# The norm's weights on ScalarE's queue, and ten warming products placed six and four

## The chip, the cores and the metric

The kernel runs on one core of a Trainium2 chip. The core has TensorE (PE in the profile; PEld is its weight load), VectorE (DVE), ScalarE (ACT), GpSimd (POOL) and SyncE (SP). SyncE only issues transfers here; ScalarE and GpSimd can issue transfers of their own besides computing. The metric is device microseconds for one execution. Three timed runs of the kernel before took 772.16, 772.48 and 773.34 us; the median is 772.48 us.

## The reference

One hybrid decoder layer on x of 256 tokens by 2048 channels, in float32. x is normed, projected by one wide matrix into two token mixers (a gated DeltaNet and an attention, eight heads of 128 each), their outputs are gated, projected, merged, projected again, normed and added to x:

```python
def rms_norm(x, w):
    y = xf * lax.rsqrt(jnp.mean(xf * xf, axis=-1, keepdims=True) + NORM_EPS)
    return (y * w.astype(jnp.float32)).astype(x.dtype)
...
    proj = h @ w_in
    gdn_qkv, gdn_z, gdn_b, gdn_a, moba_qkv, moba_z, gate_a, gate_b = jnp.split(proj, offsets, axis=-1)
...
    h = rms_norm(x, pre_norm_w[l])
    y = hybrid_mixer(h, w_in[l], conv_w[l], a_log[l], dt_bias[l], gdn_norm_w[l],
                     w_branch_a[l], w_branch_b[l], w_out[l])
    x = x + rms_norm(y, post_norm_w[l])
```

Only the first line of the layer matters for the change: `h = rms_norm(x, pre_norm_w)`, and the first columns of `h @ w_in`.

## The kernel before, in words

Every large product splits its float32 operands into a rounded part (`hi`) and the rest (`lo`), and adds three products: hi by hi, hi by lo, lo by hi. ScalarE makes `hi` with a copy, VectorE makes `lo` with a subtraction. `hT` holds the transposed and weighted x, hi in columns 0 to 255 and lo in columns 256 to 511 of each of 16 blocks of 128 channels. The factor 1/rms is applied later, to the products.

The first phase computes the first four heads' keys (`pfirst`, tiles `a_k`) straight from arriving data. Nothing has been loaded when it begins, so it runs as a pipeline over eight chunks of 256 channels (two blocks):

- SyncE's queue issues, in the order of the text: `nrow` (L162: the norm's weights, 16 rows of 128), and then for each chunk two pieces of x (L171, 128 tokens by 256 channels) and two pieces of `w_in` (L173, tile `rawf_k`, 128 channels by 512 columns). The small tables `prow` and `adrow` (L185 to L189) and the later weights (L352 on) come behind these.
- TensorE multiplies a matrix of ones with itself WARM times (L231, tile `warm`; no result is used), transposes `nrow` (L288, tile `pnc`), from which VectorE copies `ncol`, the weights as a column (L289), transposes the four x blocks of chunk 0 (L290, `turn(0)`, tile `hTp`), and multiplies the ones again WARM2 times (L291). A float32 product of 128 columns is two MATMUL rows of the trace; a transpose is one.
- `turned(c)` (L247) makes ScalarE write the hi half of a block of `hT`, scaled by `ncol` (L254), and the hi of the weights (L255), and VectorE the lo half of `hT` (L257) and the lo of the weights (L261), block by block.
- `first_products(k, part)` (L279) is four products with hi of the weights (512 columns, since hT's hi and lo lie side by side) or four with lo (256 columns). For the first two chunks, the next chunk's `turn` and `turned` stand between the first block's hi and lo products, later ahead of both (L295 to L301). `stats` sums the squares of x beside it.

`pin` (L145) keeps pinned instructions of an engine in the order of the text; every TensorE instruction is pinned, and so are the copies and subtractions of `turned` and the copy at L183, which stands at the head of ScalarE's own work. Other instructions may be placed elsewhere on their engine when the program is built. From the second phase on, `proj_t` and `proj_n` stream weights of up to 1 MB through three buffers (`wraw`), in an order written out by hand (`ORDER`), and queues of generators (`tick`) put the small work of the two mixers between the products.

```python
    for i in range(WARM):
        mm(warm[:, :P], ones, ones, start=True, stop=True)
...
    tr(pnc[:, :KT], nrow, ident[:KT, :KT])
    pin(nc.vector.tensor_copy(ncol, pnc[:, :KT]))
    pt = turn(0)
    for i in range(WARM2):
        mm(warm[:, :P], ones, ones, start=True, stop=True)
    turned(0, pt)
```

Of the kernel before, what the change touches and what calls it, by code (L numbers as in the profile page):

```python
# [15 lines left out]
P = 128  # L16
EPS = 1e-6
NEG = -1e30

WARM = 4  # L20
WARM2 = 7
STATS = 1, 2, 4, 5

PG_WAIT = 3.5
# [51 lines left out]
def hybrid_layer(  # L76
# [15 lines left out]
    nc = tc.nc  # L92
# [35 lines left out]
    def aux_tile(name):  # L128
        return aux.tile([P, 512], F32, tag="aux", name=name)
# [17 lines left out]
    def mm(*args, **kwargs):  # L147
        return pin(nc.tensor.matmul(*args, **kwargs))  # L148
# [10 lines left out]
    ZW, ZBA = ZG[3] - ZG[2], GW - ZG[2]  # L159

    nrow = cst.tile([KT, P], F32, name="nrow")
    nc.sync.dma_start(nrow, pre_norm_w.rearrange("o (k p) -> (o k) p", p=P))  # L162
    prow = big.tile([P, P], F32, tag="ga", name="prow")
    xall = big.tile([P, NT, D], F32, tag="u1", name="x")
    xs = [xall[:, t, :] for t in range(NT)]
# [64 lines left out]
    warm = aux_tile("warm")  # L230
    for i in range(WARM):  # L231
        mm(warm[:, :P], ones, ones, start=True, stop=True)
# [5 lines left out]
    def turn(c):  # L238

        pt = aux_tile(f"hTp_{c}")  # L240
        for k in range(2):
            for t in range(NT):
                f = (2 * c + k) * P
                tr(pt[:, k * S + t * P : k * S + (t + 1) * P], xs[t][:, f : f + P], ident)
        return pt
# [44 lines left out]
# [3 lines that stand above are left out]
# [1006 lines left out]
```

## Time and profile before

| what | value |
|---|---|
| median of 3 runs | 772.48 us (772.16 to 773.34) |
| the profiled execution, its own time | 773.75 us |
| its span, first to last instruction | 772.0 us |
| granted TensorE clock over the span | 0.997 |
| TensorE busy (matmuls) | 762.1 us, 99% of the span |
| VectorE, ScalarE, GpSimd busy | 565.5, 435.5, 34.9 us |
| moved by DMA | 151.87 MB, mean 197 GB/s |

The profiled execution took 773.75 us, of which 1.7 us lie outside the span; it is 1.27 us above the median of the timed runs. Times in the views count from the span's start. In a timeline row the first number is the start, the second the stretch that the merged instructions cover, both in us; "x8" is their count; the bracket gives the engine's idle time ahead and what ended it. A row "SPq" is a transfer's issue on SyncE, not the transfer. The clock column tells only what the profile records of the clock's throttle; the durations of equal instructions tell the rate that TensorE ran at.

### The profile page before, as it was taken

The numbers are of one execution on the slowest core, as the hardware profiler recorded it, in microseconds if no ns is written. First come the engines' busy times: TensorE is split into PE (matmuls) and PEld (weight loads), VectorE is DVE, ScalarE is ACT, GpSimd is POOL, SyncE is SP. The second block draws the span as 40 slices with busy tenths as digits, with TensorE's granted clock in tenths as the row PEclk, the third lists the DMA queues.
The fourth block names the chain that finished last, engine by engine and source line by source line (L and its number), as shares of the span: only waits on it lengthen the run. The fifth ranks groups of instructions, "written<-read, shape, count | busy, mean of one in ns | idle before, by whom it ended". The sixth has DMA issues, their size and how long they took to land.

```text
span 772.0 us, 10411 instructions
## 1 busy us (share of the span) xinstructions
PE 762.1 (99%) x3943; PEld 650.8 (84%) x3943; DVE 565.5 (73%) x918; ACT 435.5 (56%) x660; POOL 34.9 (5%) x63
## 2 busy tenths in 40 slices
PE   9999999999999999999999999999999999999995
PEld 8898988899888888888898888788888888888884
DVE  5887769885977898775457876686648676888843
ACT  5777666657655654554456474654455544555731
POOL 4000001112000000003001000000000000000000
PEclk9999999999999999999999999999999999999998
DMA  8576676458565557668437356667545955375912
GB/s 289 181 234 219 182 218 183 137 149 231 184 206 174 190 184 215 172 194 203 135 109 273 126 200 217 229 212 245 197 163 172 372 180 202 112 296 190 339 45 110
DMA packets 94808, 151.87 MB, mean 197 GB/s; under 512 B 3365, under 2 KB 49062, under 8 KB 94246
## 3 DMA queue, kind: packets, MB, share of 16 engines
q1 hardware_dynamic: 90054, 134.42, 53.8%
q0 software_dynamic: 4128, 15.74, 6.1%
q10 hardware_dynamic: 576, 1.05, 0.4%
q8 instruction: 31, 0.51, 0.3%
q14 instruction: 19, 0.16, 0.1%
HBM read 148.04 MB, written 3.15 MB: 196 GB/s over the span
## 4 chain that ended last, share of the span: by engine, by line
PE 96%; ACT 2%; DVE 1%; DMA 0%; issue 0%; DVEq 0%; SPq 0%
PE a_gb L148 11%; PE a_ga L148 11%; PE a_y L148 11%; PE a_zg L148 6%; PE a_k L148 6%; PE a_mq L148 6%; PE a_v L148 6%; PE a_mk L148 6%; PE a_ub L148 6%; PE a_zm L148 6%; PE a_mv L148 5%; PE a_ua L148 5%; PE a_q L148 4%; PE s L148 1%; PE ms L148 1%; PE po L148 1%
## 5 line engine op out<-in xcount | busy, mean ns | idle before, releaser
L148 PE MATMUL a_ga<-hi_ga,hT 128*128 128x512 f32 x256 | 82.1, 394 | 0.0
L148 PE MATMUL a_gb<-hi_gb,hT 128*128 128x512 f32 x256 | 80.2, 390 | 0.0
L227 DVE TENSOR_TENSOR lo_gb<-raw_gb,hi_gb 128x1024 fp32r<-128x1024 f32 x32 | 38.9, 1224 | 25.0 <-ACT hi_gb L226 24.9
L148 PEld LDWEIGHTS a_gb<-hi_gb,hT 128*128 128x128 f32 x256 | 48.0, 188 | 10.5
L148 PEld LDWEIGHTS a_ga<-hi_ga,hT 128*128 128x128 f32 x256 | 48.1, 188 | 10.1
L226 ACT CAST hi_gb<-raw_gb 128x1024 fp32r<-128x1024 f32 x32 | 33.3, 1051 | 35.6 <-PE a_gb L148 26.5
L226 ACT CAST hi_ga<-raw_ga 128x1024 fp32r<-128x1024 f32 x32 | 33.6, 1054 | 32.1 <-PE a_ga L148 13.7
L227 DVE TENSOR_TENSOR lo_ga<-raw_ga,hi_ga 128x1024 fp32r<-128x1024 f32 x32 | 38.9, 1222 | 17.4 <-ACT hi_ga L226 17.2
L148 PE MATMUL a_ga<-lo_ga,hT 128*128 128x512 f32 x128 | 50.1, 392 | 0.1
L148 PE MATMUL a_gb<-lo_gb,hT 128*128 128x512 f32 x128 | 50.1, 391 | 0.0
L148 PE MATMUL a_zg<-hi_zg,hT 128*128 128x348 f32 (+1 forms) x192 | 47.1, 322 | 0.0
L148 PE MATMUL a_mq<-hT,hi_mq 128*128 128x512 f32 x128 | 47.0, 408 | 0.0
L148 PE MATMUL a_mk<-hT,hi_mk 128*128 128x512 f32 x128 | 46.2, 402 | 0.0
L148 PE MATMUL a_y<-hi_y,mT 128*128 128x512 f32 x144 | 46.1, 392 | 0.0
L148 PE MATMUL a_q<-hT,hi_q 128*128 128x512 f32 x128 | 45.9, 398 | 0.0
L148 PE MATMUL a_v<-hT,hi_v 128*128 128x512 f32 x128 | 45.3, 399 | 0.0
L148 PE MATMUL a_k<-hT,hi_k 128*128 128x512 f32 x128 | 41.4, 407 | 0.0
L148 PE MATMUL a_ub<-hi_ub,obT 128*128 128x512 f32 x128 | 41.3, 395 | 0.0
L148 PE MATMUL a_zm<-hi_zm,hT 128*128 128x512 f32 x128 | 40.5, 392 | 0.0
L148 PE MATMUL a_mv<-hi_mv,hT 128*128 128x512 f32 x128 | 40.1, 391 | 0.0
L148 PE MATMUL a_v<-hT,lo_v 128*128 128x256 f32 x128 | 36.0, 281 | 0.0
L148 PE MATMUL a_q<-hT,lo_q 128*128 128x256 f32 x128 | 35.9, 280 | 0.0
(384 smaller groups left out, 1976.6 us busy)
## 6 DMA issues: line engine op xcount, KB each, us to landing
raw_ga<-in_w_in_dram SPq DMA_DIRECT2D x16, 1024.0 KB, 5.1
raw_gb<-in_w_in_dram SPq DMA_DIRECT2D x16, 1024.0 KB, 6.0
raw_y<-in_w_out_dram SPq DMA_DIRECT2D x15, 1024.0 KB, 5.3
raw_q<-in_w_in_dram SPq DMA_DIRECT2D x8, 1024.0 KB, 5.6
raw_mv<-in_w_in_dram SPq DMA_DIRECT2D x8, 1024.0 KB, 5.1
raw_v<-in_w_in_dram SPq DMA_DIRECT2D x8, 1024.0 KB, 5.6
raw_zm<-in_w_in_dram SPq DMA_DIRECT2D x8, 1024.0 KB, 5.0
raw_mq<-in_w_in_dram SPq DMA_DIRECT2D x8, 1024.0 KB, 5.7
```

The source lines that it names most:

```text
L148: return pin(nc.tensor.matmul(*args, **kwargs))
L226: nc.scalar.copy(hi, raw)
L227: nc.vector.tensor_tensor(lo, raw, hi.bitcast(F32), op=ALU.subtract)
```

## The change

The transfer of `nrow` is issued by ScalarE instead of SyncE, so that x's first piece is the first transfer on SyncE's queue. WARM goes from 4 to 6 and WARM2 from 7 to 4: six warming products ahead of the transposes and four behind them, ten in all instead of eleven. Nothing else is edited.

```diff
-WARM = 4
-WARM2 = 7
+WARM = 6
+WARM2 = 4
...
     nrow = cst.tile([KT, P], F32, name="nrow")
-    nc.sync.dma_start(nrow, pre_norm_w.rearrange("o (k p) -> (o k) p", p=P))
+    nc.scalar.dma_start(nrow, pre_norm_w.rearrange("o (k p) -> (o k) p", p=P))
```

## The prediction

> **What bounds the kernel now.** I read the page first (shares, chain), then TensorE's waits, the chain over the first 40 us, and last the first 14 us engine by engine.
>
> ```profile
> span 772.0 us, 10411 instructions
> PE 762.1 (99%) x3943; PEld 650.8 (84%) x3943; DVE 565.5 (73%) x918; ACT 435.5 (56%) x660; POOL 34.9 (5%) x63
> PE 96%; ACT 2%; DVE 1%; DMA 0%; issue 0%; DVEq 0%; SPq 0%
> ```
>
> TensorE is busy 99% of the span and carries 96% of the chain. Its waits over the whole run, and the head of the chain:
>
> ```profile
> PE warm L148 <- DVE epst L182: 1.1, 1, 1.1
> PE hTp L151 <- DMA x<-in_x_dram: 0.7, 1, 0.7
> ...
> 1.27 2.81 DMA x<-in_x_dram
> 4.13 1.27 PE hTp L151 x4
> 5.40 2.99 PE warm L148 x14
> 8.39 1.71 PE a_k L148 x4
> ```
>
> Only two waits stand in the list, both before 4.13 us. So what TensorE does before its first real product (`a_k`, 8.04 us below) lies on the path, and later work follows TensorE. The one stretch later on in which the chain leaves it for long runs from 50.9 to 63.9 us over ScalarE and VectorE; it begins where TensorE's products release it (chain: `a_zg` ends, `hi_q` starts) and moves along with them. Nothing behind 35 us is edited. I therefore forecast the shift of the first phase and carry it to the end undiminished.
>
> TensorE's rows of that phase, weight loads left out but for one:
>
> ```profile
> 1.14 2.08 PE L148 MATMUL warm<-ones 128*128 128x128 f32 x8 [1.14 <-DVE epst L182]
> 3.15 0.28 PE L151 MATMUL pnc<-ident,nrow 16*128 16x16 f32 x1
> 4.13 1.27 PE L151 MATMUL hTp<-ident,x 128*128 128x128 f32 x4 [0.70 <-DMA x<-in_x_dram]
> 4.50 0.50 PEld L151 LDWEIGHTS hTp<-ident,x 128*128 128x128 f32 x3 [0.19 <-DMA x<-in_x_dram]
> 5.20 3.19 PE L148 MATMUL warm<-ones 128*128 128x128 f32 x14
> 8.04 2.05 PE L148 MATMUL a_k<-hT,hi_k 128*128 128x512 f32 x4
> 9.89 0.68 PE L151 MATMUL hTp<-ident,x 128*128 128x128 f32 x4
> 10.33 0.72 PE L148 MATMUL a_k<-hT,lo_k 128*128 128x256 f32 x4
> 10.88 1.08 PE L148 MATMUL a_k<-hT,hi_k 128*128 128x512 f32 x4
> 11.80 0.64 PE L148 MATMUL a_k<-hT,lo_k 128*128 128x256 f32 x4
> 12.27 1.09 PE L148 MATMUL a_k<-hT,hi_k 128*128 128x512 f32 x4
> ...
> L148 PE MATMUL warm<-ones x22: 421/421/580, 1.1 to 8.0; 128*128 128x128 f32 x22
> ```
>
> Four hi products take 2.05 us at 8.04 and 1.08 at 10.88: TensorE runs at half rate until about 10.0 us and at full rate from there. The third hi group, at 12.27, is my marker; what it gains, the run gains. The work from the first product to the marker, at full rate, is two hi groups of 0.92 (10.88 to 11.80), two lo groups of 0.47 (11.80 to 12.27) and four transposes of 0.44 (9.89 to 10.33): 3.22 us. Check: 1.96 us at half rate do 0.98 of it, and 12.27 minus 10.0 is 2.27, together 3.25.
>
> **The change part by part.** *Warming products.* Fourteen rows span 3.19 us and one lasts 0.42, so a step is (3.19 - 0.42)/13 = 0.213 us; a product is two rows. WARM + 2 adds four rows, 0.85 us; WARM2 - 3 takes six away, 1.28 us. The four added rows would end at 3.22 + 0.85 = 4.07, so they fill the time in which TensorE now waits for x. The transpose of `nrow` comes behind them: it starts 0.07 before the last warming row ends now, so at 4.00; the first x transpose between 4.07 and 4.28 (its 0.28), I take 4.2, against 4.13 now.
>
> *The queue.* These rows price it:
>
> ```profile
> 0.82 0.39 SPq L162 DMA_DIRECT2D nrow<-in_pre_norm_w_dram  x1
> 1.27 0.88 SPq L171 DMA_DIRECT2D x<-in_x_dram  x2
> 3.14 0.91 SPq L171 DMA_DIRECT2D x<-in_x_dram  x2
> ...
> DMA to landing us min/median/max: 1.6/1.6/1.6
> ...
> DMA to landing us min/median/max: 2.8/4.2/4.9
> ...
> L1224 ACTq DMA_DIRECT2D out_dram<-yw x4: 338/338/377, 757.0 to 768.2; - x4
> ...
> 0.82 1.28 ACT L183 ACT_TABLE_LOAD   x1 [0.82 <-PEq L1285]
> 2.12 0.19 ACT L183 COPY rstd<-epst 128x2 f32<-128x2 f32 x1
> 5.44 0.47 ACT L254 ACTIVATE hT<-hTp,ncol 128x256 fp32r<-128x256 f32 x1 [3.13 <-PE hTp L151]
> 5.95 0.62 ACT L255 CAST hi_k<-rawf_k 128x512 fp32r<-128x512 f32 x1
> ```
>
> The first landing row is `nrow`'s, the second x's. Everything behind `nrow` on SyncE is issued 0.45 us earlier (1.27 - 0.82): x lands at about 3.63 and 4.0 instead of 4.08 and 4.46, so the waits of 0.70 and 0.19 go. What is late next is TensorE itself, which reaches the transposes at 4.2; so the queue's move brings the first transpose nothing that the added products don't use up, and its worth is that the second one no longer waits. On ScalarE the issue costs 0.34 to 0.38 (the ACT rows of L1224) ahead of the table load, or stands behind it. Nothing on ScalarE is wanted before 5.3, and the copy at L183 then ends at 2.7: cost nothing, cover 2.6 us. `nrow` lands at 2.4 if issued first, at 2.1 + 1.6 = 3.7 behind the table load; both are ahead of 4.00.
>
> *Sum up to the first product.* Transposes: three steps of 0.213 plus 0.42 from 4.2, end 5.26 (5.40 now). Their slot ends 0.20 earlier, so warming starts at 5.06; its eighth row at 6.55, the first product 0.07 behind it, as now: 6.62 against 8.04, 1.42 us earlier. The data allow it: ScalarE starts `hT` at 5.30, and `hi_k` (0.47 + 0.62) ends at 6.4.
>
> *The rate.* Work done at half rate before the doubling was free behind warming products; now real products take that place. If doubling stays at 10.0, 3.38 us at half rate do 1.69 of the 3.22, and the marker comes at 11.53: gain 0.74. That is one end. For the other: now TensorE works without a hole from 4.13 and doubles at 10.0, 5.9 us later. After the change it works without a hole from 1.14, so by the same 5.9 it doubles at 7.05 or before: marker at 6.62 + 3.22 + 0.43/2 = 10.05, gain 2.2. VectorE limits more than that:
>
> ```profile
> 5.95 0.48 DVE L257 SCALAR_TENSOR_TENSOR hT<-hTp,ncol,hT 128x256 fp32r<-128x256 f32 x1 [2.31 <-ACT hT L254]
> 6.59 1.19 DVE L261 TENSOR_TENSOR lo_k<-rawf_k,hi_k 128x512 fp32r<-128x512 f32 x1 [0.16 <-ACT hi_k L255]
> 7.70 0.47 DVE L257 SCALAR_TENSOR_TENSOR hT<-hTp,ncol,hT 128x256 fp32r<-128x256 f32 x1
> 8.10 1.22 DVE L261 TENSOR_TENSOR lo_k<-rawf_k,hi_k 128x512 fp32r<-128x512 f32 x1
> ```
>
> From 6.4 it needs 1.19 + 0.47 + 1.22 + 0.48 before the marker's operand exists: 9.8, so no gain passes 2.45. Chunk 1 of x, second piece, is issued at about 3.6 and lands 4.2 to 4.9 later; 0.45 earlier that is 7.35 to 8.05, wanted at about 7.7: 0 to 0.3 us, I take 0.1.
>
> Sum for the likeliest case: 2.2 - 0.1 = 2.1 against the profiled execution, 773.75 to 771.65 us (span 769.9). That execution is 1.27 above the median; the runs shown spread over 1.18 us with nothing in the program to cause it, and the moment of the doubling is the one thing seen that could differ. I take it that the median run lost 0.2 us less to the half rate: gain 1.9, 772.48 to 770.6 us.
>
> [...] The windows, with the clock in the column behind GpSimd's count:
>
> ```profile
> 8.00:10.00 2.00, 2.00 (x7) 1.51 (x7) 1.32 (x2) 0.00 (x0) 0.79 (x1) 1.00 0.97 332
> 767.00:768.00 1.00, 0.00 (x0) 0.00 (x0) 1.00 (x2) 0.00 (x0) 0.00 (x0) 0.90 0.64 238
> 768.00:769.00 1.00, 0.00 (x0) 0.00 (x0) 0.56 (x2) 0.00 (x0) 0.00 (x0) 0.50 0.99 377
> ```
>
> [...]
>
> **The rivals.** *Doubling as late as now.* Transposes or the small product of `nrow` break the run-up as the hole at 3.43 to 4.13 did. Counted from the end of the transposes, 5.2 now, doubling took 4.8 us; from 5.05 it would come at 9.9, gain 0.74: 771.7 us. For it: the transposes were part of the same disturbed stretch, so no row separates them from the hole. [...]
>
> *`nrow` becomes the wait.* Its transpose stands ahead of x's on TensorE, so `turn(0)`, `ncol` and all of `turned(0)` queue behind it. If ScalarE issues it at 2.1 and it shares the engines with x and the weights, which land after 4.2 (median), it comes at 6.3: first product at 8.9, the hole lets doubling come at 12.3, the half rate costs 1.7: marker 13.8, 1.5 us later, 774.0. It decides from a landing at 4.9 on (first product 7.5, doubling 10.9, marker 12.4). Against: 8 KB landed in 1.6 us.
>
> *Another order.* Unpinned instructions may be placed differently when the program is built; one table load of 1.28 us more or fewer in the stretch at 50.9 would turn the 770.6 into 771.9 or 769.3. For it: `hi_q` and its neighbours there aren't pinned. Against: the edit touches nothing after 10 us.
>
> **How the numbers follow.** 0.2%, 1.5 us, is about what a measurement of this kernel can tell from no change. Likeliest, early doubling: 0.52, range 769.9 to 771.3, of which 0.42 lies below 770.94. Late doubling: 0.26, same. `nrow` late: 0.14, of which 0.11 slower. Other order: 0.08, of which 0.03 faster, 0.02 slower. Faster 0.45, same 0.42, slower 0.13. The range 769.8 to 773.2 takes in late doubling and the milder half of `nrow` late.
>
> **What would show it.** In the changed profile: no wait for x at `hTp`; `pnc` at about 4.0; first product at 6.6; `nrow` issued on ACTq; the four hi products that begin there taking about 1.1 to 1.5 us, not 2.05, and the marker at 10.0 to 10.3. A marker at 11.5 is late doubling; a wait of `pnc` for `nrow` is the third case. The prediction is wrong if the marker comes early and the end does not, or if the instructions behind 35 us stand in another order.

## The result, and the profile after

| | before | after |
|---|---|---|
| median of 16 runs each, us | 772.86 (772.16 to 773.71) | 771.32 (770.50 to 772.11) |
| the profiled execution, us (its span) | 773.75 (772.0) | 772.10 (770.4) |
| first real product, us | 8.04 | 6.68 |
| marker (third hi group of `a_k`), us | 12.27 | 10.22 |

The ratio of after to before is 0.998, with a 95% interval of 0.9973 to 0.9987: 1.5 us faster, 0.2%. Forecast were 770.6 us and a gain of 1.9.

The page of after, its span and busy times, and behind them the list of TensorE's waits over the whole run:

```profile
span 770.4 us, 10406 instructions
PE 761.0 (99%) x3941; PEld 650.0 (84%) x3941; DVE 565.7 (73%) x918; ACT 435.3 (57%) x660; POOL 35.0 (5%) x63
```

```profile
PE warm L148 <- DVE epst L182: 1.1, 1, 1.1
```

The wait for x has gone from the list. TensorE's timeline of after, weight loads left out, then ScalarE's, then `nrow` in the list of transfers (the last number is the time to landing):

```profile
1.14 2.93 PE L148 MATMUL warm<-ones 128*128 128x128 f32 x12 [1.14 <-DVE epst L182]
4.00 0.28 PE L151 MATMUL pnc<-ident,nrow 16*128 16x16 f32 x1
4.21 1.11 PE L151 MATMUL hTp<-ident,x 128*128 128x128 f32 x4
5.12 1.92 PE L148 MATMUL warm<-ones 128*128 128x128 f32 x8
6.68 1.38 PE L148 MATMUL a_k<-hT,hi_k 128*128 128x512 f32 x4
...
10.22 1.10 PE L148 MATMUL a_k<-hT,hi_k 128*128 128x512 f32 x4
```

```profile
0.82 0.41 ACTq L162 DMA_DIRECT2D nrow<-in_pre_norm_w_dram  x1
1.26 1.28 ACT L183 ACT_TABLE_LOAD   x1 [1.26 <-PEq L1285]
2.56 0.19 ACT L183 COPY rstd<-epst 128x2 f32<-128x2 f32 x1
5.36 0.47 ACT L254 ACTIVATE hT<-hTp,ncol 128x256 fp32r<-128x256 f32 x1 [2.61 <-PE hTp L151]
```

```profile
nrow<-in_pre_norm_w_dram ACTq DMA_DIRECT2D x1, 8.0 KB, 2.4
```

The issue of `nrow` stands first on ScalarE and pushes the table load back by 0.44 us, into time in which ScalarE has nothing to do. `nrow` lands after 2.4 us instead of 1.6, at 3.2, ahead of the 4.00 at which it is wanted. The first four hi products take 1.38 us, partly at half rate; the trace's clock record puts the doubling at 7.12 us (10.04 before). VectorE, ScalarE and GpSimd carry the same instructions in the same order in both traces.

The marker came 2.05 us earlier, the end only 1.65. The shift stays at 2.05 up to about 180 us; the rest is lost at one place. The timelines of before and then of after show the transfers of the DeltaNet's triangles to DRAM (`l_d`) and back (`lc`), which ScalarE then copies; the line behind each is from the view of `lc`, its four transfers' time to landing; the last fence has TensorE's rows of after at that place.

```profile
180.82 2.33 POOL L508 DMA_DIRECT2D l_d<-gdn  x4 [7.74 <-DVE gdn L536]
185.00 1.97 POOL L632 DMA_DIRECT2D lc<-l_d  x4 [1.84 <-DMA l_d<-gdn]
189.61 3.16 ACT L635 COPY lc<-lc 32x1024 f32<-32x1024 f32 x3 [1.47 <-DMA lc<-l_d]
```

```profile
DMA to landing us min/median/max: 4.6/4.9/5.0
```

```profile
178.77 2.34 POOL L508 DMA_DIRECT2D l_d<-gdn  x4 [7.74 <-DVE gdn L536]
182.95 1.98 POOL L632 DMA_DIRECT2D lc<-l_d  x4 [1.84 <-DMA l_d<-gdn]
188.16 3.16 ACT L635 COPY lc<-lc 32x1024 f32<-32x1024 f32 x3 [2.07 <-DMA lc<-l_d]
```

```profile
DMA to landing us min/median/max: 5.2/5.5/5.7
```

```profile
193.32 0.28 PE L148 MATMUL a_v<-hT,lo_v 128*128 128x256 f32 x1
193.44 0.40 PE L148 MATMUL a_v<-hT,hi_v 128*128 128x512 f32 x1
193.98 0.39 PE L148 MATMUL a_v<-hT,lo_v 128*128 128x256 f32 x1
194.20 0.39 PE L148 MATMUL a_v<-hT,hi_v 128*128 128x512 f32 x1
```

The issues are 2.05 us earlier, but `lc` took 5.5 us to land instead of 4.9, so the copies are only 1.45 earlier. `hi_v` and `lo_v` stand behind them, and TensorE waits: 0.54 us from 193.44 to 193.98 and 0.22 to the next row, where such steps are elsewhere 0.24 and 0.12 long, 0.4 us in all.

### The profile page after: what moved, and what is told of

The parts are those of the page before. It is cut to its first block, busy times and chain, and to the rows that moved or that the text cites. A ratio compares the mean times of both kernels' runs of the same rounds, so it can differ in the third digit from the quotient of the medians.

```text
span 770.4 us, 10406 instructions
## 1 busy us (share of the span) xinstructions
PE 761.0 (99%) x3941; PEld 650.0 (84%) x3941; DVE 565.7 (73%) x918; ACT 435.3 (57%) x660; POOL 35.0 (5%) x63
## 4 chain that ended last, share of the span: by engine, by line
PE 94%; ACT 2%; DVE 2%; DMA 1%; issue 0%; POOL 0%; DVEq 0%; POOLq 0%
PE a_gb L148 11%; PE a_ga L148 11%; PE a_y L148 11%; PE a_mq L148 6%; PE a_mk L148 6%; PE a_k L148 6%; PE a_ub L148 6%; PE a_zm L148 6%; PE a_zg L148 5%; PE a_mv L148 5%; PE a_ua L148 5%; PE a_q L148 4%; PE a_v L148 4%; PE s L148 1%; PE ms L148 1%; PE po L148 1%
```

## The experiments

The theory under test: the time follows the marker, and the marker follows two things, the place of the first product and the moment of the doubling, which comes early only after a run-up without a hole. The rivals: that the earlier x alone is what counts; that the number of warming products behind the transposes alone counts; that transposes don't count as run-up.

**Either part alone, and a third way.** Edits against the kernel before (e1, e2, e3), and against after (e4):

```diff
 e1:  nc.scalar.dma_start(nrow, ...)   WARM = 4   WARM2 = 7
 e2:  nc.sync.dma_start(nrow, ...)     WARM = 6   WARM2 = 4
 e3:  nc.sync.dma_start(nrow, ...)     WARM = 4   WARM2 = 4
 e4:  nc.scalar.dma_start(nrow, ...)   WARM = 6   WARM2 = 0
```

> nrow on ScalarE's queue, warming products left at four and seven. My theory (the place of the first product and the moment of doubling set the time): x lands near 3.4 and 3.8 as in the changed kernel, the hole ahead of the transposes shrinks from 0.70 to about 0.2 us but the seven products behind still hold the first product back to about 7.5 (8.04 before, 6.68 in the changed kernel). Gain 0.3 to 1.0 us: 0.5 of first product less its half rate, more if the shorter hole lets doubling come early. Rival (the earlier x is what counts): nearly the whole 1.5 us, 771.3.

> nrow left on SyncE's queue, warming products six and four. My theory: x lands at 4.08 and 4.46 as before, the transposes start at 4.2 and the second waits some 0.2; first product at 6.7 to 6.8, no hole longer than 0.3, so gain within 0.3 us of the changed kernel's: 771.3 to 771.7. Rival (the earlier x is what counts): first product held by the data at 7.0 or later, gain under 0.8, 772.1 or more.

> nrow on SyncE's queue, four warming products ahead and four behind: three fewer behind the transposes and nothing to fill the wait for x. My theory: first product near 6.75, almost as early as in the changed kernel, but the hole of 0.70 stays, so doubling comes at 7.6 to 11 as in the kernel before; gain 0.6 to 0.8 us, 772.1. Rival (fewer warming products behind is all, the hole ahead is harmless): the changed kernel's gain, 771.3 to 771.5.

> The changed kernel with no warming product behind the transposes: TensorE stands idle from about 5.3 until its first product's operands exist at about 6.4. It has 1.7 us less of half-rate work. My theory (an unbroken run-up is what brings doubling early): the new hole of 1.1 us resets it, doubling comes at 9.8 to 13 instead of 4.6 to 8, the first 3.2 us of products run at half rate; 1.2 to 2.8 us slower than the changed kernel, 772.5 to 774. Rival (only the number of products ahead of the first real one counts): same as the changed kernel or up to 0.2 us faster, 771.1 to 771.3.

All four ran beside the kernel before, which had a median of 773.18 us (35 runs).

| kernel | median, us (runs) | range | ratio to before | doubling and marker in its profile, us |
|---|---|---|---|---|
| e1 queue only | 771.27 (11) | 770.90 to 773.40 | 0.998 (0.9971 to 0.9988) | 9.90, 12.01 |
| e2 products only | 771.54 (11) | 771.05 to 772.18 | 0.998 (0.9971 to 0.9989) | 4.94, 9.96 |
| e3 four and four | 772.45 (11) | 771.45 to 773.03 | 0.9989 (0.998 to 0.9997) | 9.38, 11.28 |
| e4 six and none | 771.31 (12) | 770.42 to 774.03 | 0.9987 (0.9978 to 0.9996) | 12.51, 12.57 |

e2 and e3 went as the theory said. e3 takes three products away behind the transposes and leaves the hole, which is worth 0.7 us. e2 differs from e3 only by the two products that fill the wait, and gains 1.6 us; so filling the wait brings 0.9 of it. The transposes in e3, then those of e2 with its first product:

```profile
3.71 1.53 PE L151 MATMUL hTp<-ident,x 128*128 128x128 f32 x4 [0.28 <-DMA x<-in_x_dram]
```

```profile
4.21 0.99 PE L151 MATMUL hTp<-ident,x 128*128 128x128 f32 x4
6.38 1.21 PE L148 MATMUL a_k<-hT,hi_k 128*128 128x512 f32 x4 [0.28 <-ACT hi_k L255]
```

In e3 TensorE waits 0.28 us ahead of the transposes and some 0.4 between them (1.53 us long, 1.11 in after); in e2 they run through. e3 and after reach their first product at the same time (6.69 and 6.68) and still differ by some 0.8 us of gain, so the first product's place isn't all of it.

e1 missed my 0.3 to 1.0: the queue's move alone is worth 1.9 us, and 771.27 is the time that its rival gave (771.3). The rival's reason, that the earlier x is what counts, doesn't stand all the same, since e2 gains 1.6 us without it. e1's profile shows a late execution, TensorE's rows:

```profile
3.25 0.25 PE L151 MATMUL pnc<-ident,nrow 16*128 16x16 f32 x1
3.44 0.47 PE L151 MATMUL hTp<-ident,x 128*128 128x128 f32 x1
4.11 0.90 PE L151 MATMUL hTp<-ident,x 128*128 128x128 f32 x3 [0.20 <-DMA x<-in_x_dram]
4.80 3.20 PE L148 MATMUL warm<-ones 128*128 128x128 f32 x14
7.65 2.05 PE L148 MATMUL a_k<-hT,hi_k 128*128 128x512 f32 x4
```

Doubling at 9.90 there, marker 0.26 earlier than before, and that execution took 773.4. The other ten took 770.90 to 772.39. Moving x forward shrinks the hole from 0.70 to 0.20 us of recorded idle time (0.67 between the starts of the first two transposes, 0.46 more than a step), and that seems to be short enough in most executions. That most of those ten doubled early is inferred from their times; only the late one left a trace.

e4 fell into two groups: seven runs from 770.42 to 771.33 and five from 772.93 to 774.03. The theory had named only the second; the first is where its rival stood (771.1 to 771.3). The profile is of the second group:

```profile
4.21 1.11 PE L151 MATMUL hTp<-ident,x 128*128 128x128 f32 x4
6.50 2.04 PE L148 MATMUL a_k<-hT,hi_k 128*128 128x512 f32 x4 [1.18 <-DVE hT L257]
8.35 1.05 PE L151 MATMUL hTp<-ident,x 128*128 128x128 f32 x4
9.05 1.20 PE L148 MATMUL a_k<-hT,lo_k 128*128 128x256 f32 x4
10.05 1.91 PE L148 MATMUL a_k<-hT,hi_k 128*128 128x512 f32 x4
```

TensorE works from 1.14 to 5.3, idles 1.18 us, and everything up to 12 us runs at half rate: the second hi group takes 1.91 us, where after took 1.09. In the other group, which left no trace, the doubling presumably came before the hole could spoil it. As far as these times show, then, not every execution pays for the hole: seven of twelve runs were as fast as after. What decides it was not shown.

**The yardstick, and fewer products.** Against after:

```diff
 e6:  WARM = 5    WARM2 = 3
 e7:  WARM = 6    WARM2 = 2
 e8:  LC_WAIT = 5     (3.5 in after)
```

> The changed kernel once more, as the yardstick for the three beside it. Both theories: 1.3 to 1.9 us ahead of the kernel before. In its profile my theory expects doubling between 4.6 and 8.0 us and the marker between 9.8 and 10.6; and, if the wait for lc near 194 us is a matter of chance, lc's transfers landing after anything from 4.5 to 5.7 us.

> The changed kernel with five warming products ahead and three behind. x has landed at 3.4 and 3.8 there, so five products (end 3.86) already cover it: the transposes start near 4.0, end at 5.05, and three products behind reach 6.15, just when the first product's operands exist (rawf_k lands near 5.5, hi_k ends near 6.1). My theory: first product near 6.2 instead of 6.68, no hole over 0.3, doubling as early as in the changed kernel, so 0.1 to 0.4 us faster than it. Rival (VectorE is the bound of the marker already): same within 0.1.

> The changed kernel with two warming products behind the transposes instead of four: they end near 6.2, the operands exist at 6.4, a hole of 0.2 to 0.4 us. My theory: 0.85 us less work ahead, of which a half or less shows (first product at 6.5), 0 to 0.3 us faster than the changed kernel, with now and then a late doubling. Rival (any hole resets it): 1 us or more slower, spread as wide as without any product behind.

> The changed kernel with the wait ahead of lc's copies on ScalarE lengthened (LC_WAIT 5 instead of 3.5), so that they stand some 4 us later in ScalarE's order and lc has landed by then. My theory (the 0.4 us lost at 194 us in the changed kernel's profile is lc's late landing, which holds up hi_v and lo_v behind it): no idle time of ScalarE ahead of the copies, the shift at 215 us equal to that at 180, 0.2 to 0.4 us faster than the changed kernel where lc is late and the same where it is not. Rival (the inverse that starts from lc is itself on the path): the same or slower by up to 4 us.

Before had a median of 773.01 (29 runs) beside them.

| kernel | median, us (runs) | range | ratio to before | doubling and marker in its profile, us |
|---|---|---|---|---|
| e5 after again | 771.38 (11) | 771.08 to 772.08 | 0.998 (0.9971 to 0.9989) | 6.02, 9.96 |
| e6 five and three | 771.50 (8) | 770.76 to 772.44 | 0.998 (0.997 to 0.999) | 4.94, 9.96 |
| e7 six and two | 772.95 (11) | 770.87 to 773.55 | 0.9988 (0.998 to 0.9997) | 5.53, 9.98 |
| e8 lc's copies later | 771.41 (10) | 770.78 to 772.12 | 0.9978 (0.9969 to 0.9987) | 6.46, 9.95 |

The yardstick repeats the gain (1.6 us). e7 missed its gain of 0 to 0.3 us and came out as its rival had it (1 us or more slower, widely spread): it again has two groups, five runs up to 771.41 and six from 772.95. Its profile is of the first:

```profile
5.12 0.81 PE L148 MATMUL warm<-ones 128*128 128x128 f32 x4
6.63 1.19 PE L148 MATMUL a_k<-hT,hi_k 128*128 128x512 f32 x4 [0.70 <-ACT hi_k L255]
```

That execution had doubled at 5.53, ahead of its hole of 0.70 us, and so its last warming rows were short. At half rate the four rows would end at 5.12 + 3 x 0.213 + 0.42 = 6.18; the first products of these profiles start at 6.38 to 6.63, so in an execution that hasn't doubled the hole is an estimated 0.2 to 0.45 us. No trace of the second group was kept.

e6 missed its gain of 0.1 to 0.4 us. Its profile, doubled at 4.94, has a hole in the same place:

```profile
6.39 1.21 PE L148 MATMUL a_k<-hT,hi_k 128*128 128x512 f32 x4 [0.57 <-ACT hi_k L255]
```

But its six warming rows start at 4.99 and at half rate would end at 4.99 + 5 x 0.213 + 0.42 = 6.48, so by this estimate an execution that hasn't doubled has no hole there. Of e6's runs one, at 772.44, stands apart; after had none above 772.11 in 27 runs. So two of the four products behind the transposes can't be spared (1.6 us in the median), while one fewer on either side costs and brings nothing that can be measured.

With early doubling the marker stands at 9.95 to 9.98 us in five profiles, wherever the first product stood (6.38 to 6.63): something else holds it, which e11 takes up.

e8 is undecided on its own question. In e5 and e8 `lc` landed after a median of 4.9 us and TensorE lost nothing at 194 us in either; the shift of the first phase, 2.3 us in both, reaches the end. Across the nine profiles of e1 to e8 and after, `lc`'s median lay between 4.8 and 5.5 us. In e2 it was 5.3, and there the shift of 2.3 us had been regained by 215 us. So the loss of 0.4 in after's profile is one execution's late `lc`, not a price of the change; why `lc` was late there stays open. The later copies themselves cost and brought nothing that can be measured.

**Do transposes count?** e9 makes all products of ones into transposes of ones, ten ahead and forty behind, e10 has as many rows of products (five and twenty):

```diff
-        mm(warm[:, :P], ones, ones, start=True, stop=True)
+        tr(warm[:, :P], ones, ident)          # e9, with WARM = 10, WARM2 = 40
 e10: WARM = 5   WARM2 = 20
```

> The changed kernel with its products of ones replaced by transposes of ones: ten ahead of x's transposes and forty behind, some 10 us of nothing but transposes on TensorE before the first real product. The question is whether transposes bring the doubling on. If they count as work like products (my likeliest case): doubling between 5 and 9 us, in the middle of the transposes, seen as their step going from 0.213 to 0.11 us; first product near 8 to 10. [...]

> The control for it: the changed kernel with five products of ones ahead and twenty behind, fifty rows as there. Both theories: doubling between 4.6 and 8.0 us, in the middle of the products, first product between 8 and 11.

The rows of e9, and of e10 behind them:

```profile
1.59 2.39 PE L151 MATMUL warm<-ident,ones 128*128 128x128 f32 x10 [1.59 <-POOL ident masks.py:199]
...
5.04 4.96 PE L151 MATMUL warm<-ident,ones 128*128 128x128 f32 x40
9.76 1.18 PE L148 MATMUL a_k<-hT,hi_k 128*128 128x512 f32 x4
```

```profile
4.57 4.63 PE L148 MATMUL warm<-ones 128*128 128x128 f32 x40
8.95 1.18 PE L148 MATMUL a_k<-hT,hi_k 128*128 128x512 f32 x4
```

Forty transposes at a step of 0.213 us would take 8.5 us; they took 4.96. Single rows have steps of 0.213 up to 5.9 and 0.109 behind it, and the clock record has the doubling at 5.91, before any real product. So e9's float32 transposes brought the doubling on at 5.91, as e10's products did at 4.42 (a little ahead of the 4.6 expected as the earliest; forty rows in 4.63 us). One execution of each is on record, 774.54 and 773.49 us; their long run-ups hold the first product back, to 9.76 and 8.95.

**What holds the marker.** GpSimd fills `tv`, a matrix needed at 190 us, between 2.7 and 8.8 us, beside VectorE's first subtractions. e11 is after with the fill made dependent on `rrow`:

```diff
+        nc.vector.tensor_copy(tv[:, 0, 0:1], rrow[:, 0:1])
         nc.gpsimd.memset(tv, 1.0)
```

> The changed kernel with GpSimd's fill of tv held back by a one-column copy from rrow on VectorE, so that it runs near 36 us instead of beside VectorE's first subtractions. My theory: in the executions with early doubling the marker stands at 9.96 whatever precedes it, because VectorE's first two lo_k subtractions take 1.2 to 1.4 us instead of 0.69 beside GpSimd; without that they take 0.69, the marker falls to 9.6 to 9.8, gain 0.1 to 0.3 us over the changed kernel. Rival (the marker is held by x or the weights landing): subtractions shorter, marker unmoved. Either could lose up to 0.5 us again if the fill slows VectorE near 36 us where it matters.

Its median was 771.12 us (10 runs, 770.69 to 771.63), beside 772.89 of before (14 runs): ratio 0.9977 (0.9967 to 0.9986). VectorE's timeline in after, then in e11, and last e11's marker in TensorE's timeline:

```profile
6.38 1.42 DVE L261 TENSOR_TENSOR lo_k<-rawf_k,hi_k 128x512 fp32r<-128x512 f32 x1
7.72 0.47 DVE L257 SCALAR_TENSOR_TENSOR hT<-hTp,ncol,hT 128x256 fp32r<-128x256 f32 x1
8.11 1.23 DVE L261 TENSOR_TENSOR lo_k<-rawf_k,hi_k 128x512 fp32r<-128x512 f32 x1
9.26 0.47 DVE L257 SCALAR_TENSOR_TENSOR hT<-hTp,ncol,hT 128x256 fp32r<-128x256 f32 x1
```

```profile
6.38 0.69 DVE L261 TENSOR_TENSOR lo_k<-rawf_k,hi_k 128x512 fp32r<-128x512 f32 x1
6.99 0.48 DVE L257 SCALAR_TENSOR_TENSOR hT<-hTp,ncol,hT 128x256 fp32r<-128x256 f32 x1
7.41 0.69 DVE L261 TENSOR_TENSOR lo_k<-rawf_k,hi_k 128x512 fp32r<-128x512 f32 x1
8.65 0.48 DVE L257 SCALAR_TENSOR_TENSOR hT<-hTp,ncol,hT 128x256 fp32r<-128x256 f32 x1 [0.55 <-ACT hT L254]
```

```profile
9.82 1.09 PE L148 MATMUL a_k<-hT,hi_k 128*128 128x512 f32 x4
```

Both subtractions fall to 0.69 us and VectorE waits for ScalarE instead. The marker stands at 9.82, 0.14 ahead of e5's and just behind the 9.6 to 9.8 expected; from the first product at 6.50 to there TensorE now waits for nothing, and the rows take 3.32 us. The medians of e11 and e5 differ by 0.26 us on times that spread by about 1; it is the best median of the study, but its interval overlaps after's, so a gain over after isn't shown.

## Why the prediction was right, and where a size was off

*First product.* Forecast 6.62, measured 6.68. `pnc` at 4.00 as forecast, the first x transpose at 4.21 (4.2), ScalarE's `hT` at 5.36 (5.30). The cover held: nothing on ScalarE or SyncE became late.

*Doubling.* Forecast 7.05 by the 5.9 us of unbroken work, measured 7.12 in after's profile; marker 10.22 against 10.15 (10.05 and 0.1 for x), and 2.05 us of gain there against 2.1. That agreement is partly luck: e5 doubled at 6.02, so 5.9 us is no constant; the 0.1 for x wasn't spent, since nothing waits for x there, and the rows up to the marker take 3.32 us at full rate (e11), not 3.22. Late doubling, the first of the rivals, at 0.26, is what e4's trace shows, and what the slower groups of e4 and e7 suggest; after had no run that looks like it. Its mechanism, transposes breaking the run-up, fell with e9, which doubled at 5.91 with nothing but transposes before it. No run shows what the expectations' ranges for the doubling were worked out from; measured were 4.42 (e10) to 7.12 (after) in the profiles of after, e2 and e5 to e10, 9.38 in e3, 9.90 in e1 and 12.51 in e4.

*The queue.* "Brings the first transpose nothing that the added products don't use up" held for the two together: e2 without it has 1.6 us as well. But I read the queue's own worth as only the second transpose's wait of 0.19. Alone it is worth as much as the products (e1), presumably because it shortens the same hole. The two parts do one job twice: together they gain no more than either alone, but none of 27 runs lay above 772.11, where e1 had 772.39 and 773.40.

*The limit by VectorE.* Forecast that the marker can't pass 9.8; five early executions stand at 9.95 to 9.98, and e11 moves it to 9.82. Right in kind, 0.15 short in size.

*From the profiled execution to the median.* This is the mis-sized term. I took the median run of before to be only 0.2 us better off than its profiled execution, beyond the common distance, and so forecast a gain of 1.9. Before's median is 0.89 below its profiled execution (773.75 - 772.86) and after's 0.78 below its own (772.10 - 771.32), so the gain of the medians, 1.54, is nearly that of the two profiled executions, 1.65. Of the 0.72 us between 770.6 and 771.32 the smaller gain makes up half; the other half is before's own median, 772.86 over 16 runs and not the 772.48 of three. After's profiled execution took 0.85 more than e5's (771.25): a marker 0.26 later, the loss of 0.4 at `lc`, and 0.2 more that builds up in TensorE's rows between about 490 and 600 us, for a reason that stays open. Before's 0.89 would need doubling near 8 us in its typical execution if that were all of it; no second profile of before was taken, so this stays open. *Carried to the end undiminished* held in e2, e5, e6, e7 and e8 (first-phase shifts of 2.3 us, ends 2.4 to 2.6 earlier than before's profile) and failed by 0.4 in after's own profile, at `lc`.

*The time by itself decides little.* The range of 769.8 to 773.2 took in late doubling (771.7) as well; 771.32 lies closer to that than to 770.6, while the gain of 1.54 lies closer to 1.9 than to 0.74. That the doubling came early is shown by the traces of after and e5, not by the time.

*The other rivals.* `nrow` landed at 3.2, so it never was the wait; the order of the other engines is unchanged.

## What to carry to other kernels

At the head of this kernel a wait of TensorE cost more than its length: some 0.7 us of idle time put the doubling of the rate off (9.38 us in e3 with it, 4.94 in e2 without it), so that real products ran at half rate (the first four took 2.07 us in e3, 1.21 in e2). Two products in its place brought 0.9 us (e2 against e3), and shortening it by 0.5 brought 1.9 (e1). Fill the wait with work that needs no data or shorten it by issuing the first needed transfer first; one of the two sufficed here. Cutting warming work behind it paid while no new hole opened (e3, three products fewer: 0.7 us), and that hole has to be worked out for an execution still at half rate (e7, two fewer than after: 1.6 us lost in the median). Judge such an edit by many runs, since one execution of the same kernel can show either side (e4's lie between 770.42 and 774.03).

## What the runs showed that was not expected

The distance from the doubling to the halving at the end, in the clock records of thirteen traces (before, after, e1 to e11), takes four values: 757.76 us in six, 761.17 in five, and 754.35 and 764.59 in one each. They lie 3.41 us apart ((764.59 - 754.35)/3 = 3.413), and each is a whole number of such steps: 222, 223, 221 and 224. In after the halving shows near the end (the clock column is the third from the right; 0.94 puts it at 764.88):

```profile
764.00:765.00 1.00, 0.00 (x0) 0.00 (x0) 0.96 (x3) 0.00 (x0) 0.00 (x0) 0.94 0.00 0
765.00:766.00 1.00, 0.00 (x0) 0.00 (x0) 1.00 (x3) 0.00 (x0) 0.00 (x0) 0.50 0.37 131
```

The doubling itself moves from execution to execution: after doubled at 7.12, the same kernel in e5 at 6.02. Nor did every gap put it off. e6 doubled at 4.94 although its first two transposes start 0.34 us more than a step of 0.213 apart (3.79 and 4.34); e1, with 0.46 more in the same place, doubled at 9.90. How long a gap may be was not shown.
